# A two-block transformer kernel: residual spread over tiles, later products, fewer mask passes

## The chip, the cores and the metric

The kernel runs on one core of a Trainium2 chip as one launch. The metric is the device time of the launch in microseconds. Engines are named as in the profile: PE (matrix products), DVE, ACT, POOL (elementwise work) and SP (which issues the DMA transfers).

## The reference

Everything is float32, with 1024 rows of width 1024. Two blocks follow each other.

```python
# block 1
mod = silu(c) @ w_mod + b_mod            # six vectors: sh1, sc1, g1, sh2, sc2, g2
z = (x*(1+sc1) + sh1) @ w_in             # feeds four mixers
y = concat(mlstm(z), sgu(z), conv(z), s5(z)) @ w_out
x = layer_norm(ALPHA*x + g1*y, ln1_w, ln1_b)
x = layer_norm(ALPHA*x + g2*swiglu(x*(1+sc2)+sh2), ln2_w, ln2_b)   # hidden width 2816
# block 2
proj = rms_norm(x) @ w_in_2              # 3512 columns
ret  = group_norm(retention(q, k, v)) * silu(r_g)          # 8 heads of 64
sel  = top_k(indexer_score(i_q, i_k, i_w), 256)            # per query, causal by chunks of 64
dsa  = softmax over the selected keys, 8 heads, latent keys/values, * silu(d_g)
x = x + concat(ret, dsa) @ w_out_2
x = x + sigmoid(rms_norm(x) @ w_ple_gate) * (p @ w_ple_proj)
out = rms_norm(x)
```

The S5 mixer is a complex linear recurrence in both directions over 16 groups of 16 channels. Where more than 256 keys can be seen by a query, those with the 256 highest indexer scores count, ties going to the lower key.

## The kernel before

Each float32 product is made of three PE products of split operands (high by high, low by high, high by low): lines 184 to 186 for one order of operands and 195 to 197 for the other. `k.split` makes the two parts of a weight page: the high part on ACT (L173), the low part, `raw - high`, on DVE (L174). Weights arrive in 3 `raw` buffers; 46 pages of 128 x 1024 float32 serve all other tiles; PSUM has 4 banks in a pool `mm` and 4 in a pool `ax`.

The program is written as Python generators. `merge` and `pipe` run them a step at a time, and a `yield` ends a step; so the place of an instruction in the program follows from the number of yields before it. A scheduler then orders the instructions of each engine by their place in the program, and may run a later one first where the earlier is not ready.

**Stage A (0 to about 640 us)** works out the modulation vectors, the mixers and LN1. `mod_rest` adds up eight products of a `w_mod` page by a scalar on DVE (`macc`, L1317) and then sums over partitions on PE with a column of ones (L1324), for four vectors. Each of the 16 `s5_group`s multiplies on PE, scans and rotates on DVE and POOL, makes `sr` and `si` (L2147, L2148) on DVE, ends its step, and adds three products on PE (L2153 to L2155). `s5_groups` loads T for each quad of groups and LO and E for each half quad just before they are used.

**Stage B (640 to 1350)** is the FFN. `Ffn.half(j, h)` makes hidden tile j for half h of the rows. In blocks of two hidden tiles, `stage_b` makes the halves, multiplies the rows of w_ffn_out by g2 on POOL (L395), splits them, and adds their products to the eight tiles `acc[t]` of the stream (PE L184 to L186 into `ax`, DVE L429). After block 0's weights, the eight tiles are turned into the residual: L407 multiplies by `ALPHA*ln1_w` on DVE, L408 adds `ALPHA*ln1_b` on DVE and POOL in turns; both vectors are loaded and scaled (L402, L405) just before.

**Stage C (1350 to 2160)** is block 2. `retention_pair` (L870 to L915) makes for each tile t a projection in an `mm` bank, rotates it on DVE and POOL (`rA`), transposes it on PE into an `ax` bank (L888, L889), and makes scores (`st`, two `ax` banks), output (`po`, L906/L907) and state (`pn`), one `ax` bank each. Behind it, as background work, `search` finds each query's 256th score by bisection on DVE (L763) and ACT, and the mask loop turns scores into 0 or 1e30 for tiles 2 to 7, in six steps of passes over the tile, all on DVE: L803 (count over a threshold), L805 and L806 (least score at or under it), L813 (count again), L816 (equal), L818 (running count), L820, L821 and L823 (the mask). The sparse attention of a tile (`head`) makes logits (L1149, L1150) plus mask (L1151), exponentials, transposes (L1161), and the value products L1177 for two heads at a time (`AVB = 2`), at the end of every second head.

Of the kernel before, what the change touches and what calls it, by code (L numbers as in the profile page):

```python
# [10 lines left out]
F32 = mybir.dt.float32  # L11
# [40 lines left out]
AVB = 2  # L52
# [319 lines left out]
def stage_b(k, ffn, acc, mod_s, ln1_w, ln1_b, w_fo, ln2_w, ln2_b, x2_s, sink, early, pre_sink, after, background, spare):  # L372
# [3 lines left out]
    FB = 2  # L376
    for b0 in range(0, NF, FB):
# [3 lines left out]
        for j in blk:  # L381
            for h in range(2):
                if j or h:
                    for _ in ffn.half(j, h):
                        pass
            acts.append(ffn.a.pop(j))
            del ffn.w[j]
        if b0 == 0:
            g2b = page("g2b")
            k.bcast(g2b, mod_s, 5120, 1024)  # L390
# [8 lines left out]
        if b0 == 0:  # L399
            aw = page("aw")  # L400
            k.bcast(aw, ln1_w, 0, 1024)
            nc.gpsimd.tensor_scalar(aw, aw, ALPHA, None, op0=ALU.mult)  # L402
            ab = page("ab")
            k.bcast(ab, ln1_b, 0, 1024)
            nc.gpsimd.tensor_scalar(ab, ab, ALPHA, None, op0=ALU.mult)  # L405
            for t in range(8):
                nc.vector.tensor_tensor(acc[t], acc[t], aw, op=ALU.mult)  # L407
                (nc.vector if t % 2 else nc.gpsimd).tensor_tensor(acc[t], acc[t], ab, op=ALU.add)  # L408
# [43 lines left out]
BIG = 1.0e30  # L452
MAGIC = 12582912.0
# [58 lines left out]
class StageC:  # L512
# [223 lines left out]
    def search(self):  # L736
# [7 lines left out]
        act_tiles = {2, 3, 4, 5}  # L744
# [48 lines left out]
    def masks(self):  # L793

        k, nc, n_sel, th = self.k, self.k.nc, 256, self.th
        for j, t in enumerate(range(2, 8)):
# [6 lines left out]
            nc.vector.tensor_scalar(a[:, :w], x, T, None, op0=ALU.is_gt, op1=ALU.add, accum_out=c[:, 0:1])  # L803
            yield 1
            nc.vector.tensor_scalar(a[:, :w], x, T, 3.0e38, op0=ALU.is_le, op1=ALU.mult)  # L805
            nc.vector.tensor_tensor_reduce(e[:, :w], x, a[:, :w], 1.0, 3.0e38, op0=ALU.add, op1=ALU.min, accum_out=c[:, 1:2])  # L806
            yield 1

            nc.vector.tensor_scalar(c[:, 2:3], c[:, 0:1], n_sel - 0.5, None, op0=ALU.is_gt)
            v = k.sm.tile([128, 1], F32, name="tkv", bufs=2)  # L810
            nc.vector.tensor_copy(v, T)
            nc.vector.copy_predicated(v, c[:, 2:3].bitcast(I32), c[:, 1:2])
            nc.vector.tensor_scalar(a[:, :w], x, v, None, op0=ALU.is_gt, op1=ALU.add, accum_out=c[:, 0:1])  # L813
            nc.vector.tensor_scalar(c[:, 3:4], c[:, 0:1], -1.0, float(n_sel), op0=ALU.mult, op1=ALU.add)
            yield 1
# [1518 lines left out]
```

## Time and profile before

| | |
|---|---|
| time, median of 3 runs | 2163.7 us (2162.11 to 2166.16) |
| the profiled execution | 2162.43 us, span 2160.4 us |
| PE busy | 2027.2 us, 94% of the span |
| DVE, ACT, POOL busy | 1291.4, 790.5 and 403.4 us |
| mean granted PE clock | 0.972 |

The span is what the profiler saw of the engines; the other 2.0 us of the profiled execution lie around it. A row of the timeline gives the start, the duration, the engine, the line, and in square brackets how long the engine had idled before and what ended that. A row of the waits is a sum over the whole run.

### The profile page before, as it was taken

What the parts mean: (1) busy time and instruction counts of PE and PEld (TensorE: products, weight loads), DVE (VectorE), ACT (ScalarE), POOL (GpSimd) and SP (SyncE); (2) the same over time, 40 slices, a digit from 0 to 9 for tenths busy, and PEclk for the clock granted to TensorE, in tenths of its full rate; (3) what the DMA queues carried; (4) which work ended last, traced back from release to release, by engine and by line L of the source; (5) the groups of instructions that cost most, each with busy time, mean ns of one, the idle gap of its engine ahead of it and who ended that gap; (6) DMA issues with size and microseconds to landing.
All of it is one profiled execution on the core that took longest, in us unless ns stands there. A gap on an engine that the chain in (4) does not pass through costs nothing. (4 is left out here: it accounts for less than half of the span.)

```text
span 2160.4 us, 29069 instructions
## 1 busy us (share of the span) xinstructions
PE 2027.2 (94%) x10808; PEld 1671.3 (77%) x10808; DVE 1291.4 (60%) x2652; ACT 790.5 (37%) x1570; POOL 403.4 (19%) x455
## 2 busy tenths in 40 slices
PE   8897898899997999999999999999999897999998
PEld 3797887777876888888887788786777785778886
DVE  6967725476666534555346454757888556966533
ACT  2522224343131222222222221545887434345432
POOL 1464403112024000000000001430002121000032
PEclk9999899989999999999999999999999998999999
DMA  8464564356411235554335543313312205343611
GB/s 288 158 161 144 149 194 166 129 167 219 171 49 59 100 113 200 187 202 162 128 140 205 186 160 116 142 40 108 142 50 89 88 24 161 133 151 115 222 59 69
DMA packets 144334, 299.32 MB, mean 139 GB/s; under 512 B 30648, under 2 KB 70072, under 8 KB 144192
## 3 DMA queue, kind: packets, MB, share of 16 engines
q1 hardware_dynamic: 144192, 297.46, 40.8%
q8 instruction: 85, 1.39, 0.3%
q14 instruction: 57, 0.47, 0.1%
HBM read 208.81 MB, written 87.56 MB: 137 GB/s over the span
## 5 line engine op out<-in xcount | busy, mean ns | idle before, releaser
L195 PE MATMUL mm<-hh,whi 128*128 128x512 f32 x704 | 275.2, 391 | 5.0 <-ACT whi L173 5.0
L197 PE MATMUL mm<-hh,wlo 128*128 128x512 f32 x704 | 274.9, 390 | 0.9 <-DVE wlo L174 0.9
L196 PE MATMUL mm<-hl,whi 128*128 128x512 f32 x704 | 274.9, 390 | 0.0
L184 PE MATMUL mm<-whi,xTh 128*128 128x512 f32 (+1 forms) x576 | 227.9, 400 | 2.9 <-DMA whi<-scr_wsp 1.7
L185 PE MATMUL mm<-wlo,xTh 128*128 128x512 f32 (+1 forms) x576 | 226.0, 394 | 0.8 <-DMA wlo<-scr_wsp 0.8
L186 PE MATMUL mm<-whi,xTl 128*128 128x512 f32 (+1 forms) x576 | 224.5, 393 | 0.0
L174 DVE TENSOR_TENSOR wlo<-raw,whi 128x1024 fp32r<-128x1024 f32 (+2 forms) x99 | 121.7, 1249 | 126.4 <-ACT whi L173 126.0
L395 POOL TENSOR_TENSOR raw<-raw,g2b 128x1024 f32<-128x1024 f32 x22 | 55.1, 2506 | 595.9 <-DMA raw<-in_w_ffn_out 552.5
L195 PEld LDWEIGHTS mm<-hh,whi 128*128 128x128 f32 x704 | 132.6, 188 | 33.1 <-ACT whi L173 5.9
L184 PE MATMUL mm<-whi,hhi 128*128 128x256 f32 (+1 forms) x512 | 150.6, 294 | 5.0 <-DVE csg L1515 3.4
L197 PEld LDWEIGHTS mm<-hh,wlo 128*128 128x128 f32 x704 | 132.5, 188 | 29.2 <-DVE wlo L174 1.9
L196 PEld LDWEIGHTS mm<-hl,whi 128*128 128x128 f32 x704 | 132.6, 188 | 27.5
L184 PE MATMUL ax<-whi,ah 128*128 128x512 f32 x352 | 138.4, 395 | 15.2 <-DVE acc L429 15.2
L186 PE MATMUL mm<-whi,hlo 128*128 128x256 f32 (+1 forms) x512 | 148.8, 292 | 1.9 <-POOL hlo L1359 1.5
L185 PE MATMUL mm<-wlo,hhi 128*128 128x256 f32 (+1 forms) x512 | 149.0, 291 | 0.0
L429 DVE TENSOR_TENSOR acc<-ax,acc 128x512 f32<-128x512 f32 x176 | 116.3, 684 | 38.8 <-PE ax L186 38.2
L185 PE MATMUL ax<-wlo,ah 128*128 128x512 f32 x352 | 138.0, 392 | 0.0
L186 PE MATMUL ax<-whi,al 128*128 128x512 f32 x352 | 137.9, 392 | 0.0
L367 DVE TENSOR_TENSOR sg<-mm,sg 128x512 f32<-128x512 f32 x44 | 30.4, 691 | 170.4 <-PE mm L197 159.6
L173 ACT ACTIVATE whi<-raw 128x1024 fp32r<-128x1024 f32 (+2 forms) x99 | 100.7, 1046 | 85.1 <-DMA raw<-in_w_fi_o 62.9
L184 PEld LDWEIGHTS mm<-whi,xTh 128*128 128x128 f32 x576 | 109.1, 190 | 27.9 <-DMA whi<-scr_wsp 3.7
L185 PEld LDWEIGHTS mm<-wlo,xTh 128*128 128x128 f32 x576 | 109.5, 190 | 20.2 <-DMA wlo<-scr_wsp 1.4
(615 smaller groups left out, 4476.0 us busy)
## 6 DMA issues: line engine op xcount, KB each, us to landing
raw<-in_w_fi_o SPq DMA_DIRECT2D x44, 512.0 KB, 5.6
wmr<-in_w_mod SPq DMA_DIRECT2D x32, 512.0 KB, 6.4
raw<-in_w_in_2o SPq DMA_DIRECT2D x24, 512.0 KB, 5.4
scr_wsp<-phi SPq DMA_DIRECT2D x24, 512.0 KB, 3.8
scr_wsp<-plo SPq DMA_DIRECT2D x24, 512.0 KB, 4.2
whi<-scr_wsp SPq DMA_DIRECT2D x24, 512.0 KB, 6.1
wlo<-scr_wsp SPq DMA_DIRECT2D x24, 512.0 KB, 6.7
raw<-in_w_ffn_out SPq DMA_DIRECT2D x22, 512.0 KB, 3.7
```

Source lines behind the costliest of these rows:

```text
L173: nc.scalar.activation(hi, raw, AF.Copy)
L174: nc.vector.tensor_tensor(lo, raw, hi, op=ALU.subtract)
L184: nc.tensor.matmul(ps, ah, bh, start=k == 0, stop=False)
L185: nc.tensor.matmul(ps, ah, bl, start=False, stop=False)
L186: nc.tensor.matmul(ps, al, bh, start=False, stop=k == n - 1)
L195: nc.tensor.matmul(ps, ah, bh, start=k == 0, stop=False)
L196: nc.tensor.matmul(ps, ah, bl, start=False, stop=False)
L197: nc.tensor.matmul(ps, al, bh, start=False, stop=k == n - 1)
L367: nc.vector.tensor_tensor(sg, pu, sg, op=ALU.mult)
L395: nc.gpsimd.tensor_tensor(raw, raw, g2b, op=ALU.mult)
L429: nc.vector.tensor_tensor(v[:, cs], ps, v[:, cs], op=ALU.add)
```

## The change

Seven places change:

- `stage_b`: the residual moves into a generator, `residual()`, that is stepped while block 0's halves are made (three steps in each of the three halves, whose products are yielded in pieces of 2 for that). All eight additions are on POOL; `aw` and `ab` are loaded first.
- `s5_group`: one more step before the products L2153 to L2155.
- `mod_rest`: `2 * MR` (6) units of steps before the sum L1324.
- `s5_groups`: T, LO and E are loaded one group ahead.
- the mask loop: for tiles 6 and 7 the first count and the search for the least score are left out (the threshold is used as it is); for all tiles the equality pass goes to POOL and yields 2^100, and the last three passes become two, so 5 passes for two tiles and 7 for four.
- `AVB` is 4: the value products of four heads follow each other.
- `retention_pair`: the transposed tile `pt` is in `mm`, not in `ax`.

```diff
--- before.py
+++ after.py
@@ -49,7 +49,7 @@
 RA, RB = 2, 1
 WQ, KEYS = 3, 6
 HA, HB, OA, OB = 2, 3, 4, 3
-AVB = 2
+AVB = 4
 RETS = [(0, 1), (0, 4), (0, 7), (1, 2), (1, 5), (2, 0), (2, 3), (2, 6)]
 DSAS = [(4, 4), (5, 0), (5, 4), (6, 0), (6, 4), (7, 0), (7, 2)]
 LOADS = {(3, 0): 1, (3, 2): 1, (3, 4): 1, (3, 6): 1, (7, 1): 1, (7, 3): 1, (7, 5): 1, (7, 7): 1}
@@ -374,6 +374,20 @@
     nc, page = k.nc, k.page
     NF = DFF // 128
     FB = 2
+
+    def residual():
+
+        aw, ab = page("aw"), page("ab")
+        for p, w in ((aw, ln1_w), (ab, ln1_b)):
+            k.bcast(p, w, 0, 1024)
+            nc.gpsimd.tensor_scalar(p, p, ALPHA, None, op0=ALU.mult)
+        yield 1
+        for t in range(8):
+            nc.vector.tensor_tensor(acc[t], acc[t], aw, op=ALU.mult)
+            nc.gpsimd.tensor_tensor(acc[t], acc[t], ab, op=ALU.add)
+            yield 1
+
+    res = residual()
     for b0 in range(0, NF, FB):
         blk = list(range(b0, min(NF, b0 + FB)))
         last = blk[-1] == NF - 1
@@ -381,10 +395,13 @@
         for j in blk:
             for h in range(2):
                 if j or h:
-                    for _ in ffn.half(j, h):
-                        pass
+                    for n, _ in enumerate(ffn.half(j, h, 8 if b0 else 2)):
+                        if b0 == 0 and n % 3 == 0:
+                            next(res, None)
             acts.append(ffn.a.pop(j))
             del ffn.w[j]
+        for _ in res:
+            pass
         if b0 == 0:
             g2b = page("g2b")
             k.bcast(g2b, mod_s, 5120, 1024)
@@ -396,16 +413,6 @@
             hl = page("whi", F32R), page("wlo", F32R)
             k.split(*hl, raw)
             wf.append(hl)
-        if b0 == 0:
-            aw = page("aw")
-            k.bcast(aw, ln1_w, 0, 1024)
-            nc.gpsimd.tensor_scalar(aw, aw, ALPHA, None, op0=ALU.mult)
-            ab = page("ab")
-            k.bcast(ab, ln1_b, 0, 1024)
-            nc.gpsimd.tensor_scalar(ab, ab, ALPHA, None, op0=ALU.mult)
-            for t in range(8):
-                nc.vector.tensor_tensor(acc[t], acc[t], aw, op=ALU.mult)
-                (nc.vector if t % 2 else nc.gpsimd).tensor_tensor(acc[t], acc[t], ab, op=ALU.add)
         if b0:
             for _ in range(PS):
                 next(spare, None)
@@ -450,6 +457,7 @@
 
 
 BIG = 1.0e30
+OFF = 2.0 ** 100
 MAGIC = 12582912.0
 TWO_PI = 2.0 * math.pi
 
@@ -741,7 +749,7 @@
             nc.gpsimd.memset(self.sc[t], 0.0)
             nc.gpsimd.memset(self.sc[t][:64, t * 128 + 64:], BIG)
         tl = list(range(2, 8))
-        act_tiles = {2, 3, 4, 5}
+        act_tiles = self.act_tiles = {2, 3, 4, 5}
         key = k.ctile([128, 6], "tkey", I32)
         xm = k.ctile([128, 6], "txor", I32)
         thr = k.ctile([128, 6], "tthr")
@@ -800,27 +808,29 @@
             a = k.page("tka")
             e = k.page("tke")
             c = k.sm.tile([128, 4], F32, name="tkc", bufs=2)
-            nc.vector.tensor_scalar(a[:, :w], x, T, None, op0=ALU.is_gt, op1=ALU.add, accum_out=c[:, 0:1])
-            yield 1
-            nc.vector.tensor_scalar(a[:, :w], x, T, 3.0e38, op0=ALU.is_le, op1=ALU.mult)
-            nc.vector.tensor_tensor_reduce(e[:, :w], x, a[:, :w], 1.0, 3.0e38, op0=ALU.add, op1=ALU.min, accum_out=c[:, 1:2])
-            yield 1
-
-            nc.vector.tensor_scalar(c[:, 2:3], c[:, 0:1], n_sel - 0.5, None, op0=ALU.is_gt)
-            v = k.sm.tile([128, 1], F32, name="tkv", bufs=2)
-            nc.vector.tensor_copy(v, T)
-            nc.vector.copy_predicated(v, c[:, 2:3].bitcast(I32), c[:, 1:2])
-            nc.vector.tensor_scalar(a[:, :w], x, v, None, op0=ALU.is_gt, op1=ALU.add, accum_out=c[:, 0:1])
-            nc.vector.tensor_scalar(c[:, 3:4], c[:, 0:1], -1.0, float(n_sel), op0=ALU.mult, op1=ALU.add)
-            yield 1
-            nc.vector.tensor_scalar(e[:, :w], x, v, None, op0=ALU.is_equal)
+            if t in self.act_tiles:
+                nc.vector.tensor_scalar(a[:, :w], x, T, None, op0=ALU.is_gt, op1=ALU.add, accum_out=c[:, 0:1])
+                yield 1
+                nc.vector.tensor_scalar(a[:, :w], x, T, 3.0e38, op0=ALU.is_le, op1=ALU.mult)
+                nc.vector.tensor_tensor_reduce(e[:, :w], x, a[:, :w], 1.0, 3.0e38, op0=ALU.add, op1=ALU.min, accum_out=c[:, 1:2])
+                yield 1
+
+                nc.vector.tensor_scalar(c[:, 2:3], c[:, 0:1], n_sel - 0.5, None, op0=ALU.is_gt)
+                v = k.sm.tile([128, 1], F32, name="tkv", bufs=2)
+                nc.vector.tensor_copy(v, T)
+                nc.vector.copy_predicated(v, c[:, 2:3].bitcast(I32), c[:, 1:2])
+            else:
+                v = T
+
+            nc.gpsimd.tensor_scalar(e[:, :w], x, v, OFF, op0=ALU.is_equal, op1=ALU.mult)
+            nc.vector.tensor_scalar(a[:, :w], x, v, None, op0=ALU.is_le, op1=ALU.add, accum_out=c[:, 0:1])
+            nc.vector.tensor_scalar(c[:, 3:4], c[:, 0:1], OFF, (n_sel - w) * OFF, op0=ALU.mult, op1=ALU.add)
+            yield 1
             z = k.zero1.to_broadcast([128, w])
             nc.vector.tensor_tensor_scan(x, e[:, :w], z, 0.0, op0=ALU.add, op1=ALU.add)
             yield 1
             nc.vector.scalar_tensor_tensor(x, x, c[:, 3:4], e[:, :w], op0=ALU.is_le, op1=ALU.mult)
-            nc.vector.tensor_tensor(x, x, a[:, :w], op=ALU.add)
-            yield 1
-            nc.vector.tensor_scalar(x, x, -BIG, BIG, op0=ALU.mult, op1=ALU.add)
+            nc.vector.scalar_tensor_tensor(x, a[:, :w], OFF, x, op0=ALU.mult, op1=ALU.subtract)
             self.done.add(('mask', t))
             yield 1
 
@@ -884,7 +894,7 @@
             ts = slice(t * 128, t * 128 + 128)
             nc.scalar.activation(sg[:, ts], ps[:, 384:512], AF.Silu, scale=self.rr[:, t:t + 1])
             yield from steps(RA)
-            pt = k.ax.tile([128, 2, 128], F32, name="ax")
+            pt = k.mm.tile([128, 2, 128], F32, name="mm")
             nc.tensor.transpose(pt[:, 0], qk[:, 0:2].rearrange("p h d -> p (h d)"), k.ident)
             nc.tensor.transpose(pt[:, 1], qk[:, 2:4].rearrange("p h d -> p (h d)"), k.ident)
             nc.scalar.activation(qt[:, 0], pt[:, 0], AF.Copy, scale=0.125)
@@ -1318,6 +1328,7 @@
                 yield MR
             o = k.page("mro")
             nc.sync.dma_start(o[:1], dap(I['b_mod'], cb * 1024, [[0, 1], [1, 1024]]))
+            yield 2 * MR
             for g in range(2):
                 cs = slice(g * 512, g * 512 + 512)
                 ps = k.ax.tile([128, 512], F32, name="ax")
@@ -2106,18 +2117,28 @@
 
     def s5_groups(self):
         k, nc, S = self.k, self.k.nc, self.S
-        py = {}
-        for q in range(4):
-            T = k.page("s5T", shape=[128, 848])
-            nc.sync.dma_start(T, dap(S['seq'], q * 960, [[16, 8], [3840, 16], [1, 848]]))
-            for hf in range(2):
-                LO = k.page("s5LO", shape=[128, 2, 2, 2, 128])
-                nc.sync.dma_start(LO.rearrange("p a i g c -> p (a i g c)"), dap(S['s5lo'], (q * 2 + hf) * 131072, [[1024, 128], [1, 1024]]))
-                E = k.page("s5E", shape=[128, 2, 2, 192])
-                nc.sync.dma_start(E.rearrange("p g i x -> p (g i x)"), dap(S['s5e'], (q * 4 + hf * 2) * 384, [[6144, 128], [1, 768]]))
-                for g2 in range(2):
-                    g = hf * 2 + g2
-                    yield self.s5_group(q, g, LO[:, 0, :, g2], LO[:, 1, :, g2], T[:, g * 240:g * 240 + 128], E[:, g2], py)
+        py, T = {}, {}
+
+        def load(n):
+            q, hf = divmod(n, 2)
+            if hf == 0:
+                T[q] = k.page("s5T", shape=[128, 848])
+                nc.sync.dma_start(T[q], dap(S['seq'], q * 960, [[16, 8], [3840, 16], [1, 848]]))
+            LO = k.page("s5LO", shape=[128, 2, 2, 2, 128])
+            nc.sync.dma_start(LO.rearrange("p a i g c -> p (a i g c)"), dap(S['s5lo'], (q * 2 + hf) * 131072, [[1024, 128], [1, 1024]]))
+            E = k.page("s5E", shape=[128, 2, 2, 192])
+            nc.sync.dma_start(E.rearrange("p g i x -> p (g i x)"), dap(S['s5e'], (q * 4 + hf * 2) * 384, [[6144, 128], [1, 768]]))
+            return LO, E
+
+        ahead = load(0)
+        for n in range(8):
+            q, hf = divmod(n, 2)
+            LO, E = ahead
+            for g2 in range(2):
+                g = hf * 2 + g2
+                if g2 and n < 7:
+                    ahead = load(n + 1)
+                yield self.s5_group(q, g, LO[:, 0, :, g2], LO[:, 1, :, g2], T[q][:, g * 240:g * 240 + 128], E[:, g2], py)
 
     def s5_group(self, q, g, L, O, T, e, py):
         k, nc = self.k, self.k.nc
@@ -2147,6 +2168,7 @@
         nc.vector.tensor_tensor(sr, d[:, 0], d[:, 1], op=ALU.add)
         nc.vector.tensor_tensor(si, sp[:, 1], sp[:, 0], op=ALU.subtract)
         yield 1
+        yield 1
         if g == 0:
             py[q] = k.mm.tile([128, 4, 128], F32, name="mm")
         p = py[q]
```

## Rows read from the trace of the kernel before

**Rows 1.** The page, part 1: busy us, share of the span, instructions.

```profile
PE 2027.2 (94%) x10808; PEld 1671.3 (77%) x10808; DVE 1291.4 (60%) x2652; ACT 790.5 (37%) x1570; POOL 403.4 (19%) x455
```

**Rows 2.** Windows: start:end, us, busy us of each engine (instructions), PEclk, DMA share, GB/s.

```profile
180.00:210.00 30.00, 21.96 (x152) 19.40 (x151) 24.29 (x48) 6.82 (x9) 14.42 (x19) 1.00 0.55 158
...
1800.00:1900.00 100.00, 86.59 (x433) 65.73 (x434) 79.20 (x181) 39.43 (x95) 6.47 (x3) 0.88 0.53 179
...
1920.00:2040.00 120.00, 119.42 (x911) 99.56 (x912) 72.50 (x191) 59.39 (x113) 4.17 (x4) 1.00 0.42 138
```

**Rows 3.** Waits of PE over the run: us in total, times, longest us.

```profile
PE ax L184 <- DVE acc L429: 15.2, 3, 12.0
PE mm L2154 <- DVE s5A L2147: 12.5, 8, 2.2
PE ax L888 <- DVE ro L907: 9.0, 5, 4.7
PE ax L1324 <- DVE macc L1317: 7.0, 2, 6.0
...
PE ax L2127 <- DMA s5LO<-scr_s5lo: 0.8, 3, 0.4
```

**Rows 4.** Timeline of PE, FFN block 0.

```profile
698.02 0.80 PE L184 MATMUL ax<-whi,ah 128*128 128x512 f32 x1 [11.96 <-DVE acc L429]
...
701.56 0.40 PE L184 MATMUL ax<-whi,ah 128*128 128x512 f32 x1
701.79 0.40 PE L185 MATMUL ax<-wlo,ah 128*128 128x512 f32 x1
```

**Rows 5.** Timeline of SP, DVE and POOL around the residual.

```profile
614.88 26.78 SPq L394 DMA_DIRECT2D raw<-in_w_ffn_out  x2
...
654.89 0.69 DVE L367 TENSOR_TENSOR sg<-mm,sg 128x512 f32<-128x512 f32 x1 [8.87 <-PE mm L197]
...
669.33 3.72 POOL L402 TENSOR_SCALAR aw<-aw 128x1024 f32<-128x1024 f32 x1 [15.57 <-DMA aw<-in_ln_w]
...
673.08 6.52 DVE L407 TENSOR_TENSOR acc<-acc,aw 128x1024 f32<-128x1024 f32 x3 [2.68 <-POOL aw L402]
679.52 1.21 DVE L408 TENSOR_TENSOR acc<-acc,ab 128x1024 f32<-128x1024 f32 x1
```

**Rows 6.** Timeline of PE at the other stalls and at one value burst.

```profile
229.48 0.49 PE L2154 MATMUL mm<-s5LO,s5A 128*128 128x128 f32 x2 [2.15 <-DVE s5A L2147]
...
359.80 3.57 PE L1324 MATMUL ax<-macc,ones 128*1 128x512 f32 x4 [6.04 <-DVE macc L1317]
...
1701.75 0.45 PE L888 MATMUL ax<-ident,rA 128*128 128x128 f32 x1 [4.72 <-DVE ro L907]
...
1869.77 0.80 PE L186 MATMUL mm<-whi,yohl 128*128 128x512 f32 x1 [2.35 <-DVE yohl L1115]
...
2024.16 1.97 PE L1177 MATMUL ax<-L,V 128*64 128x128 f32 x32
```

**Rows 7.** Timeline of DVE, mask passes of tiles 6 and 7.

```profile
1867.37 1.75 DVE L820 SCALAR_TENSOR_TENSOR score<-score,tkc,tke 128x896 f32<-128x896 f32 x1
...
1879.77 1.27 DVE L803 TENSOR_SCALAR_CACHE_REDUCE tka<-score,tth 128x1024 f32<-128x1024 f32 x1
...
1883.30 1.21 DVE L806 CUSTOM_DVE_ANT_0 tke<-score,tka 128x1024 f32<-128x1024 f32 x1
...
1887.38 0.75 DVE L816 TENSOR_SCALAR tke<-score,tkv 128x1024 f32<-128x1024 f32 x1
```

**Rows 8.** Single lines: duration in ns, min/median/max, first and last start.

```profile
L407 DVE TENSOR_TENSOR acc<-acc,aw x8: 1211/3356/3410, 673.1 to 694.0; 128x1024 f32<-128x1024 f32 x8
...
L408 POOL TENSOR_TENSOR acc<-acc,ab x4: 2637/3188/3247, 675.9 to 693.1; 128x1024 f32<-128x1024 f32 x4
```

**Rows 9.** Line L1177: durations as in 8; idle of its engine before it, us, times.

```profile
L1177 PEld LDWEIGHTS ax<-L,V x576: 132/137/231, 1819.3 to 2047.1; 128*64 128x64 f32 x192
...
  issue: 6.7, 28
```

## The prediction

> **What bounds the kernel now.** I read the page's first part first: PE is busy for 2027.2 of 2160.4 us and no other engine for more than 60% [rows 1]. So PE sets the end, and a change that leaves PE's products as they are can win only what PE loses: 133 us of idle time, and the time in which it runs at the lower of its two clock levels behind a gap. Then the windows, to see where this lies: 13 us between 1800 and 1900 at a granted clock of 0.88, 8 us in the 30 us from 180, and next to nothing (0.6 us) in the 120 us from 1920 [rows 2]. Then PE's waits, which name who was late: DVE, in all four of the largest waits that the change touches, 43.7 us together [rows 3]. Last the timeline at the places themselves, for what comes ahead of the late instruction and what the clock does behind the gap [rows 4 to 7]. The reader is to see that DVE is never full for long, but that its queue is in order: a pass of 1 to 3 us at the wrong moment makes PE wait.
>
> **The residual (FFN block 0).** PE stands for 11.96 us before the first output product that needs a free `ax` bank; the bank comes free when DVE adds into `acc`, and DVE is busy with L407 and L408 until then [rows 4, 5]. Behind the gap the clock is at the lower level: the eight products from 698.02 take 3.54 us, where two neighbours at the higher level start 0.23 us apart [rows 4]; eight of those are 1.84, so 1.7 us more. Some 13.6 us can be had. The change moves the 16 passes ahead, into the time of the three halves, where DVE has little to do (an idle stretch of 8.87 us ends at 654.89 [rows 5]). What it adds: nothing in passes, but four additions move from DVE at 1.21 us [rows 5] to POOL at 3.19 us [rows 8]. POOL then has, in the 36 us between the end of the transposes at about 633 and 669, where it began before [rows 5]: eight additions at 3.19 (25.5 us), two scalings at 3.72 at most (7.4 us), two products of weights, priced as additions (6.4 us): 39.3 us. It is full and overruns by some 3.3 us. Everything in POOL's queue behind an addition waits with it: the products `raw * g2b`, then the splits on DVE and ACT, then block 0's output products. SP's queue: `aw` and `ab` are now issued ahead of the two weight loads that hold SP from 614.88 to 641.66 [rows 5], so they land early. I take -10 us: 13.6 less the overrun. Bounds: -13.6 (all hidden) and +4 (a new stall of one add in front of each of the two low parts that L174 makes, and of the weights' product).
>
> DVE's L407 takes 1.21 us alone and 3.36 us at the median, beside POOL's additions [rows 8]: the two take turns. The Trainium skill says so too (GPSIMD Engine Reference, section 8, Key points): POOL shares its SBUF interfaces with DVE and gets in the way of DVE instructions with two SBUF operands, and elementwise work is about twice as fast on DVE. By that rule the four additions moved to POOL speak against this part; by the row they cost POOL's time only as long as DVE has slack.
>
> **S5 products a step later.** PE waits 12.5 us in eight waits for L2147 [rows 3], the worst kind as in [rows 6]: 2.15 us, and the DVE rows ahead of it are scans. One step more lets PE take other products first. Bounds: -12.5, and 0 if PE has nothing else or the next thing is as late. In this stretch PE is busy 21.96 us of 30 and DVE 24.29 [rows 2]: DVE is close behind as a limit, so a wait that goes here may reappear at the next DVE result. I take a third: -4.
>
> **Modulation sums later.** The two waits for `macc` are 7.0 us, one of them 6.04 [rows 3, 6], and the four sums behind it are slow too (3.57 us). After 6 more units DVE's last L1317 should be done. Who waits for the sum: DVE's L1325 and a transfer to memory, needed first much later. Bounds -7.0 and 0, taken: -4, since DVE's queue can be late by more than the step.
>
> **S5 loads ahead.** LO is last in three short waits, 0.8 us together [rows 3]. I take -1; +4 if the pages that are held longer (three of 46 for a half quad) make another load late; SP's queue is in order, so a load that waits for a page holds those behind it.
>
> **Mask passes.** At tile 7 DVE loses L803 (1.27), L805 (one operand, priced as L816 at 0.75), L806 (1.21), L816 (0.75, to POOL), and of the last three passes one (L823, priced as L816): 4.7 us [rows 7]. Tile 6, by its width, 4.1 us. Tiles 2 to 5 lose L816 and one of the last passes, 1.5 us at full width; their widths sum to 2.25 of 1024: 3.4 us. Together 12.2 us of DVE time, none of it on PE. What PE gets: the 13.4 us lost in 1800 to 1900 [rows 2] hold 2.35 us of direct wait behind L818 and L820 (1.75 us beside a POOL pass) and the low clock after it [rows 6, 7]. Added: the equality pass on POOL; no such row. Below, 0.75 us as on DVE; above, 3.72 us as L402 [rows 5, 7]. It is nearest to L402 (one operand, a scalar, POOL). Over the six widths (4.125 of 1024) that is at most 15.3 us, and if DVE stood still for all of it, 3.1 us worse than before. The scan waits for it; `e` is not needed by anything else, and L813 fills part of the wait. I take -5, bounds -12.2 and +3.1.
>
> **Value products of four heads.** Ahead of its bursts the engine idles 6.7 us in 28 cases with no releaser named [rows 9], 0.24 us a burst: 16 bursts fewer give 3.8 us, in a stretch where PE is never idle [rows 2]. A burst of 32 products is 1.97 us [rows 6]; now two such follow each other, and logits for the next head come 2 us later. Four pages are held instead of two. I take -4, bounds -4 and +4.
>
> **`pt` in `mm`.** L888 waits for L907 because both want an `ax` bank: 9.0 us, with one wait of 4.72 and the lower clock behind it, as in [rows 4] ([rows 3, 6]). In `mm` the wait for L907 goes, but `pt` and the projections then share four banks, and PE can be fewer tiles ahead. Taken: -2; bounds -11 (9.0 and 2 for the clock) and +5, one such wait more.
>
> **Sum**: -10 -4 -4 -1 -5 -4 -2 = -30, from the profiled execution's 2162.4 us (2160.4 of span and 2.0 around it) 2132.4. The median of the runs shown is 1.3 us above that execution, so 2133.7, rounded 2134. Bounds that could hold together: the low ends of the four largest parts (-13.6, -12.5, -12.2, -11) cannot all be had.
>
> **Rivals.**
> - *The residual's stall comes back* (0.13). POOL is full in 633 to 669; if the weights' low parts are queued behind the adds, PE waits there instead. Against it: DVE's idle rows. +4 in place of -10: 2134 + 14 = 2148.
> - *Stage A is bound by DVE* (0.10): DVE at 24.29 of 30 beside PE's 21.96 [rows 2]. The 9 us of S5 and modulation don't reach the end: 2143.
> - *POOL and DVE take turns in the masks* (0.12): +3.1 in place of -5: 2142. The 1.75 us of L820 beside a POOL pass speaks for it [rows 7]. The Trainium skill's page named above says elementwise work is better on DVE; by it this rival is the likely course, and the trace agrees as far as L407 shows it.
> - *`mm` is short in retention* (0.10), the one that ends slower. 32 items each have a projection and a `pt` in four banks; if each waits as the five waits for L907 do on average, 1.8 us, that is 58 us: 2134 + 2 + 58 = 2194. It decides from 0.9 us an item (28 us) on. Against it: a projection's bank is read within the same step.
> - *More than the sum* (0.05): stalls go with their low clock: about 2118.
>
> **How the numbers follow.** The forecast holds with 0.50; its own range is 2124 to 2144. The first three rivals end at 2142 to 2148; two of them together reach 2155 to 2157. A change is told from none at 0.2%, 4.3 us. Faster: 0.50 + 0.13 + 0.10 + 0.12 + 0.05 less 0.06 for rivals that come together, 0.84. Same: 0.06 and a hundredth of the slower rival, 0.07. Slower: 0.09. The range for 8 in 10 reaches from 2113 (below the fifth rival) to 2165 (rivals together, and the start of the fourth).
>
> **What would show it.** No wait of PE at `ax` for L429 in FFN block 0 and granted clock 1.0 there; waits for L2147 and `macc` gone from the list; L1177 in groups of up to 64; DVE's busy time 12 us down, POOL's 16 to 28 us up (12.8 of additions and 3 to 15 of passes); PE's busy time about the same and its idle time down by 30 us. The prediction is wrong if a wait for `wlo`, for `mm` at a projection, or for the new POOL pass appears with more than 5 us in total, or if PE's busy time rises, since then the clock took back what the waits gave.

## The result and the profile after

| | before | after |
|---|---|---|
| time, median | 2162.9 us (2162.1 to 2166.2, 4 runs) | 2136.3 us (2131.8 to 2141.3, 4 runs) |
| ratio, 95% interval | | 0.9875 (0.9849 to 0.9900) |
| profiled execution, span | 2162.4, 2160.4 us | 2141.3, 2139.5 us |
| PE, DVE, POOL busy | 2027.2, 1291.4, 403.4 us | 2019.0, 1281.4, 429.0 us |

The kernel is faster by 26.6 us at the medians. The time forecast was 2134, the measured one is 2136.3. The profiled execution is the slowest of the four; the same kernel run again gave 2135.2 us (2134.6 to 2137.7) where the kernel before took 2167.3 beside it, ratio 0.9857 (0.9841 to 0.9873), and its profiled execution has a span of 2132.9.

The waits of PE after, in us in total, times and longest:

```profile
PE ax L2148 <- DMA s5LO<-scr_s5lo: 15.3, 4, 7.2
...
PE ax L184 <- ACT whi L173: 5.7, 1, 5.7
...
PE ax L184 <- DVE acc L436: 3.2, 2, 2.6
...
PE mm L2177 <- DVE s5A L2169: 1.6, 2, 0.8
...
PE ax L1335 <- DVE macc L1327: 0.9, 1, 0.9
...
PE mm L2176 <- DVE s5A L2168: 0.3, 1, 0.3
```

Of the four waits in [rows 3] that the change was to remove, three are nearly gone: L2154's (now L2176) from 12.5 to 0.3 us, with 1.6 us at the product behind it (L2177), L888's for `ro` (L907) from the list altogether, L1324's (now L1335) from 7.0 to 0.9. The first, for `acc`, fell from 15.2 to 3.2: the one of 12.0 in FFN block 0 is gone, and the two that are left stand behind the FFN's last product of a hidden tile, with 3.2 us before as after. Two are new at the head: 15.3 us for the S5 loads, and 5.7 us for weights in FFN block 0. Over the whole span PE idles for 120.5 us instead of 133.2 (117.9 in the second execution) and is busy for 8.2 us less (12.2 in the second); its mean granted clock is 0.971 (0.973), where it was 0.972.

FFN block 0 after, PE, POOL and DVE (compare [rows 4, 5]), then the weight products on POOL before:

```profile
661.82 0.39 PE L197 MATMUL mm<-hh,wlo 128*128 128x512 f32 x1
667.87 2.07 PE L184 MATMUL ax<-whi,ah 128*128 128x512 f32 x4 [5.67 <-ACT whi L173]
...
671.20 0.63 PE L184 MATMUL ax<-whi,ah 128*128 128x512 f32 x1
...
674.50 0.40 PE L185 MATMUL ax<-wlo,ah 128*128 128x512 f32 x1
...
634.97 6.55 POOL L387 TENSOR_TENSOR acc<-acc,ab 128x1024 f32<-128x1024 f32 x2
644.49 2.71 POOL L387 TENSOR_TENSOR acc<-acc,ab 128x1024 f32<-128x1024 f32 x1 [2.96 <-DVE acc L386]
648.42 16.01 POOL L387 TENSOR_TENSOR acc<-acc,ab 128x1024 f32<-128x1024 f32 x5 [1.23 <-DVE acc L386]
664.40 4.65 POOL L412 TENSOR_TENSOR raw<-raw,g2b 128x1024 f32<-128x1024 f32 x2
...
644.87 14.55 DVE L386 TENSOR_TENSOR acc<-acc,aw 128x1024 f32<-128x1024 f32 x5
```

```profile
649.01 4.74 POOL L395 TENSOR_TENSOR raw<-raw,g2b 128x1024 f32<-128x1024 f32 x2 [16.32 <-DMA g2b<-scr_mod]
```

The gap is 5.67 us instead of 11.96, and another operand ends it: `whi`, made from `raw * g2b` (L412), which POOL takes up at 664.40, behind the last of its eight additions. Before the change POOL did these weight products first, from 649.01, and the additions later. The eight additions take 2.7 to 3.4 us each, DVE's multiplications beside them 2.9 (14.55 us for five); POOL's own work from the first scaling (629.32) to the second weight product (669.05) is 35.5 us, and for 4.2 us it waits for DVE's multiplications. PE has run out of products of hidden tiles at 662.2; before the change they lasted to 686.1. The products behind the gap are at the lower clock again (0.63 us long; 0.40 from 674.50), now for 6.6 us, where it was 3.5 [rows 4].

The masks after, the new pass on POOL and DVE's scan behind it:

```profile
1832.45 3.28 POOL L825 TENSOR_SCALAR tke<-score,tth 128x896 f32<-128x896 f32 x1
1838.87 3.71 POOL L825 TENSOR_SCALAR tke<-score,tth 128x1024 f32<-128x1024 f32 x1 [3.14 <-DVE tkc L827]
...
1839.00 2.86 DVE L830 TENSOR_TENSOR_SCAN score<-tke,zero 128x896 f32<-128x896 f32 x1
...
1848.23 2.28 DVE L830 TENSOR_TENSOR_SCAN score<-tke,zero 128x1024 f32<-128x1024 f32 x1
```

The equality pass takes 3.71 us at 1024 columns, five times the 0.75 that DVE took for the comparison alone [rows 7] (0.74 for the whole pass, in experiment 10), and the scan that runs beside it 2.86 us at 896 columns, where it took 1.97 before the change. A tile keeps four passes on DVE (tiles 6 and 7) or seven (the others), and each has one on POOL: 5 and 8 in all, where the list of the change has 5 and 7.

**Stretches.** Whole times differ from run to run by more than most parts are worth. So I read each part from the stretch in which it acts, between two events that every version has; the windows below start and end there. Stage A is read from the first S5 product (L2127 before) to the last LN1 transposition (L334), the FFN from there to the last product of a hidden tile (L197), the retention from the first to the last transposition at L888, and the attention from there to the last value product. Kernels that do not differ in a stretch agree within 1.4 us in the attention and within 2.6 in the FFN and the retention: the FFN is 706.32 us in both executions of the changed kernel, but 704.1 in the one of experiment 4; before the change it is 710.6, and 708.2 in that of experiment 5. A part of under 3 us can't be read there from one execution. Stage A is 468.4 to 468.9 us in four kernels that have none of the changes to it, and 456.6 to 462.3 in those that have all three as in the change.

### The profile page after: what moved, and what is told of

Same layout as the page of the kernel before. It is cut to its first block, busy times and chain, and to the rows that moved or that the text cites. A ratio compares the mean times of both kernels' runs of the same rounds, so it can differ in the third digit from the quotient of the medians.

```text
span 2139.5 us, 29059 instructions
## 1 busy us (share of the span) xinstructions
PE 2019.0 (94%) x10808; PEld 1673.6 (78%) x10808; DVE 1281.4 (60%) x2620; ACT 785.4 (37%) x1568; POOL 429.0 (20%) x465
## 5 line engine op out<-in xcount | busy, mean ns | idle before, releaser
L197 PE MATMUL mm<-hh,wlo 128*128 128x512 f32 x704 | 275.1, 391 | 1.4 <-DVE wlo L174 1.4
L185 PE MATMUL mm<-wlo,xTh 128*128 128x512 f32 (+1 forms) x576 | 225.2, 392 | 2.5 <-DMA wlo<-scr_wsp 2.5
L186 PE MATMUL mm<-whi,xTl 128*128 128x512 f32 (+1 forms) x576 | 223.7, 391 | 0.0
L174 DVE TENSOR_TENSOR wlo<-raw,whi 128x1024 fp32r<-128x1024 f32 (+2 forms) x99 | 126.0, 1293 | 129.4 <-ACT whi L173 128.7
L412 POOL TENSOR_TENSOR raw<-raw,g2b 128x1024 f32<-128x1024 f32 x22 | 54.1, 2463 | 597.2 <-DMA raw<-in_w_ffn_out 569.6
L197 PEld LDWEIGHTS mm<-hh,wlo 128*128 128x128 f32 x704 | 132.5, 188 | 30.0 <-DVE wlo L174 2.7
L186 PE MATMUL mm<-whi,hlo 128*128 128x256 f32 (+1 forms) x512 | 149.6, 293 | 1.9 <-POOL hlo L1370 1.5
L186 PE MATMUL ax<-whi,al 128*128 128x512 f32 x352 | 138.3, 393 | 0.0
L185 PEld LDWEIGHTS mm<-wlo,xTh 128*128 128x128 f32 x576 | 109.3, 190 | 22.5 <-DMA wlo<-scr_wsp 3.6
```

Of the source, the lines that this page charges most:

```text
L174: nc.vector.tensor_tensor(lo, raw, hi, op=ALU.subtract)
L185: nc.tensor.matmul(ps, ah, bl, start=False, stop=False)
L186: nc.tensor.matmul(ps, al, bh, start=False, stop=k == n - 1)
L197: nc.tensor.matmul(ps, al, bh, start=False, stop=k == n - 1)
L412: nc.gpsimd.tensor_tensor(raw, raw, g2b, op=ALU.mult)
```

## The experiments

**1. The changed kernel again.** No edit.

> The changed kernel once more, unaltered. It was 26.6 us under the kernel before at the medians, while its profiled execution, the slowest of its four, was 21 us under it and stood 15.3 us for S5's LO loads. Theory L (the spread of the changed kernel's runs, 2131.8 to 2141.3, is the LO wait, which varies with when the loads land): this profile has another sum for that wait, and its span follows it roughly one for one. Rival: the wait is again 14 to 16 us and the span differs for another reason. Time expected: 2136, with 2131 to 2141 as its runs' spread.

Measured: 2135.2 us; LO waits 14.1 us where they were 15.3, span 2132.9 where it was 2139.5. Theory L falls: the wait moved by 1.2 us and the span by 6.6. Some 3.3 us of it lie before the first S5 product (165.1 against 161.8 us), in the opening, and 2.7 us between it and the last LN1 transposition (windows under experiments 2 to 4). What makes this spread was not tried.

**2 to 4. S5's two parts, alone and together taken out.** No loads ahead (`no_d`), no later products (`no_b`), neither (`no_bd`), the edit shortened:

```diff
-        ahead = load(0)                  # no_d, no_bd: T, LO and E loaded
+            T = k.page("s5T", ...)       #   in the loop, just ahead of use
...
         yield 1
-        yield 1                          # no_b, no_bd
         if g == 0:
             py[q] = k.mm.tile(...)
```

> The changed kernel with S5's loads where they were before (just ahead of the half quad that uses them); the later products stay. Theory D (the loads a group ahead make the LO waits, since SP issues in order and a load that waits for a page holds the next): PE's waits for LO fall from 15.3 us to under 3, time about 8 us under the changed kernel, near 2128. Rival B (the products a step later make them, by keeping the pages of S5 longer): the waits for LO stay above 8 us, and the time is the same or some us more, 2136 to 2145.

> The changed kernel with S5's products where they were before (one step earlier); the loads a group ahead stay. Theory D (loads ahead make the LO waits): LO waits stay above 8 us, and the waits for L2147's result (12.5 us before) come back beside them, so the time is 5 to 10 us more than the changed kernel's, 2141 to 2146. Rival B (the later products make the LO waits): LO waits under 3 us, waits for sr and si near 12 us, time within 4 us of 2136.

> The changed kernel with S5 as before: products a step earlier, loads just ahead of use. Theory X (what the later products won, 12.5 us of waits for sr and si, the waits for LO took back, so both parts together are worth nothing): time 2133 to 2138, as the changed kernel. Rival S (they still bring a good part of what stage A gained, the modulation sums the rest): 2140 to 2145.

Measured: without the loads ahead 2136.3 us (ratio 0.9856), without the later products 2138.3 (0.9871), without both 2145.1 (2142.9 to 2154.2; ratio 0.9914, 0.9898 to 0.9930). The stretch from the first S5 product to the last LN1 transposition, in this order: before, after, after again, no loads ahead, no later products, neither (start and end, length, busy us of PE, PEld, DVE, ACT, POOL, clock, DMA share, GB/s):

```profile
161.50:630.27 468.77, 424.57 (x2641) 371.63 (x2640) 301.54 (x626) 140.34 (x256) 122.17 (x157) 0.94 0.48 156
...
165.10:626.82 461.72, 419.89 (x2641) 370.78 (x2640) 302.31 (x626) 137.74 (x254) 120.59 (x157) 0.94 0.50 160
...
161.80:620.86 459.06, 419.18 (x2641) 370.34 (x2640) 302.61 (x626) 137.47 (x254) 120.67 (x157) 0.94 0.50 161
...
163.70:624.17 460.47, 423.03 (x2641) 373.19 (x2640) 302.01 (x626) 140.88 (x257) 123.98 (x157) 0.94 0.50 162
...
166.50:627.29 460.79, 420.89 (x2641) 369.21 (x2640) 300.39 (x626) 137.56 (x254) 123.37 (x157) 0.95 0.49 160
...
167.20:636.24 469.04, 425.57 (x2641) 371.86 (x2640) 302.88 (x626) 140.37 (x256) 122.37 (x157) 0.95 0.49 159
```

Neither part: 469.0, as before the change (468.8). Either one: 460.5 or 460.8. Both: 461.7 and 459.1. And PE's waits without the loads ahead, without the later products, and without both:

```profile
PE ax L2138 <- DMA s5LO<-scr_s5lo: 8.1, 2, 7.3
PE mm L2166 <- DVE s5A L2158: 6.8, 5, 2.8
...
PE ax L2148 <- DMA s5LO<-scr_s5lo: 9.5, 4, 5.3
...
PE mm L2175 <- DVE s5A L2168: 2.7, 3, 1.7
...
PE mm L2165 <- DVE s5A L2158: 12.6, 9, 2.4
...
PE ax L2138 <- DMA s5LO<-scr_s5lo: 1.8, 2, 1.6
```

So theory D and rival B both fall: each part alone has LO waits of 8 to 10 us, and both together 14 to 15. Theory X falls as well: with neither there is 12.6 us of waiting for `sr` and hardly any for LO, with both the reverse, and yet both are worth 8 us of the stretch and about 10 of the time. In the length of the stage the two parts are substitutes, one is enough. A sum of waits does not tell what they are worth; part of it (2.5 to 6.4 us) is in PE's busy time (425.6 against 419.2 to 423.0).

The stretch, cut at the last S5 product (L2155 before), shows that they win in different places (us):

| | to the last S5 product | from there on |
|---|---|---|
| before | 107.6 | 361.2 |
| neither | 109.9 | 359.2 |
| loads ahead alone (`no_b`) | 95.5 | 365.3 |
| later products alone (`no_d`) | 111.3 | 349.2 |
| both (the two executions) | 105.2, 105.2 | 356.5, 353.9 |

The loads ahead shorten the first piece, in which PE idles for 14.1 us instead of 19.6, and the later products the second, 18.2 us instead of 24.6. Why the two gains do not add up is not settled.

**5. Modulation sums alone.** The kernel before with one line more:

```diff
+            yield 2 * MR
             for g in range(2):
                 cs = slice(g * 512, g * 512 + 512)
```

> The kernel before with the sums of the modulation vectors six units later, nothing else. Reading Z (from the changed kernel without S5's two parts, whose stage A from the first S5 product to the end of the transpositions is as long as before, 469.0 against 468.8 us): the waits for macc go from 7.0 to 3 us or less and nothing is won, because the time is given back at other waits for DVE in the stage; time within 2 us of the kernel before. Reading of the prediction: 4 us less, both in this stretch and in the time.

Measured: ratio 1.0001 (0.9988 to 1.0013). The waits for `macc` went from 7.0 to 2.6 us, and the stretch of stage A became longer, 472.6 us against 468.8, which is outside the 468.4 to 468.9 of kernels without this part. That is one execution, though: the kernel of experiment 4, which has the later sums too, has 469.0. The stretch and two of its waits:

```profile
164.00:636.63 472.63, 429.20 (x2641) 374.55 (x2640) 302.42 (x626) 140.32 (x256) 123.80 (x157) 0.94 0.48 155
...
PE mm L2155 <- DVE s5A L2148: 12.0, 8, 2.4
...
PE ax L1325 <- DVE macc L1317: 2.6, 1, 2.6
```

Reading Z holds here: by itself this part wins nothing.

**6. Additions shared.** The changed kernel, the residual's additions on DVE and POOL in turns, as they had been before:

```diff
             nc.vector.tensor_tensor(acc[t], acc[t], aw, op=ALU.mult)
-            nc.gpsimd.tensor_tensor(acc[t], acc[t], ab, op=ALU.add)
+            (nc.vector if t % 2 else nc.gpsimd).tensor_tensor(acc[t], acc[t], ab, op=ALU.add)
```

> The changed kernel with the residual's additions on DVE and POOL in turns, as before the change, and all else as changed. Theory P (POOL's queue sets the gap that is left in FFN block 0: the products of w_ffn_out by g2 start at 664.4, behind the last addition, and PE stands 5.7 us for the parts made of them): POOL has four additions of 2.7 to 3.2 us less, the weight products start 6 us or more earlier, the gap is under 1 us, time about 7 us under the changed kernel. Rival T (DVE and POOL take turns on the same tiles, so what POOL sheds DVE pays): the gap stays above 4 us and the time within 3 us of the changed kernel's.

Measured: 2125.6 us (2124.0 to 2131.7), ratio 0.9813 (0.9798 to 0.9828), some 10 us under the changed kernel on the same chip. PE and POOL at the gap, then the FFN's stretch before, after and in this kernel:

```profile
661.96 0.50 PE L185 MATMUL ax<-wlo,ah 128*128 128x512 f32 x1 [2.71 <-DVE wlo L174]
...
631.01 3.23 POOL L387 TENSOR_TENSOR acc<-acc,ab 128x1024 f32<-128x1024 f32 x1
...
653.52 6.71 POOL L412 TENSOR_TENSOR raw<-raw,g2b 128x1024 f32<-128x1024 f32 x2
```

```profile
630.27:1340.85 710.58, 692.68 (x3038) 571.51 (x3037) 342.43 (x412) 172.82 (x229) 75.13 (x30) 0.99 0.43 151
...
626.82:1333.14 706.32, 694.61 (x3037) 572.36 (x3037) 341.88 (x408) 172.94 (x229) 86.26 (x34) 0.99 0.43 150
...
622.86:1325.32 702.46, 693.82 (x3038) 571.94 (x3037) 347.74 (x412) 173.04 (x229) 74.81 (x30) 0.99 0.43 151
```

Theory P holds, rival T does not: with four additions instead of eight, POOL takes up the weight products 22.5 us after its first addition where it took 29.4 (653.52 less 631.01; 664.40 less 634.97), and the gap is 2.71 us, now at the low part on DVE, so not under 1 us as the theory had it. The FFN is 8.1 us shorter than before instead of 4.3. The theory expected about 7 us in the time; of the 10 measured 3.9 are in the FFN. Where the rest of the difference in time is, the trace does not tell: the profiled execution was this kernel's slowest.

**7. Masks alone.** The kernel before with the mask loop of the change (the hunks from `OFF` to the end of the loop).

> The kernel before with the mask passes alone changed (5 or 7 of 9, the equality pass on POOL). The changed kernel is 10.7 us shorter between its first and last value product than the kernel before. Theory M (as predicted: DVE's passes are what PE stands for between 1800 and 1900): this stretch is 5 to 8 us shorter, and so is the time, near 2160 where the kernel before takes 2165. Rival V (the bursts of value products carry nearly all of it): the stretch is under 2 us shorter. Rival T (POOL and DVE take turns): the stretch is longer by 1 to 3 us.

**8. Value products alone.** The kernel before with `AVB = 4`.

> The kernel before with the value products of four heads following each other, and nothing else changed. Theory of the prediction: a quarter of a microsecond for each of 16 bursts that go, 3.8 us; nothing from other effects; so the stretch from the first scores of the attention to the last value product is 3.5 to 4.5 us shorter, and the time 4 us. Rival V (fewer switches also spare waits for the transposed pages): 6 to 9 us. Rival H (four pages held and longer bursts make the logits late): 0 or longer.

Measured: masks 2162.3 us, ratio 0.9989 (0.9978 to 0.9999), values 2158.0, ratio 0.9969 (0.9954 to 0.9984). The expectations named the first value product and the first scores as boundaries, but with bursts of four heads the first value product comes 4.3 us later by itself; so both are read on one stretch, from the last retention transposition to the last value product. Before, masks alone, values alone, the changed kernel (its second execution):

```profile
1785.37:2047.52 262.15, 244.11 (x1618) 194.83 (x1618) 178.10 (x418) 119.59 (x250) 15.62 (x13) 0.95 0.47 155
...
1786.69:2044.76 258.07, 240.70 (x1618) 193.20 (x1618) 166.99 (x388) 119.56 (x250) 29.38 (x18) 0.96 0.47 158
...
1786.26:2042.32 256.06, 235.73 (x1618) 192.65 (x1618) 176.52 (x418) 118.74 (x250) 16.55 (x13) 0.95 0.48 159
...
1766.79:2020.32 253.53, 236.27 (x1618) 194.69 (x1618) 166.60 (x388) 118.30 (x250) 30.30 (x18) 0.94 0.49 160
```

Masks 4.1 us (DVE's busy time there 11 us less, POOL's 14 more); values 6.1; both in the changed kernel 8.6. Where it is, by line, in that stretch (busy us and mean ns of one; idle us before), before and then values alone:

```profile
L186 PE MATMUL mm<-whi,yohl 128*128 128x512 f32 x120 | 48.3, 408 | 2.4 <-DVE yohl L1115 2.4
L1177 PE MATMUL ax<-L,V 128*64 128x128 f32 x576 | 46.7, 282 | 1.3 <-DVE L L1166 0.8 <-ACT L L1164 0.5
L1161 PE MATMUL ax<-ident,L 128*128 128x128 f32 x288 | 45.0, 280 | 3.8 <-ACT L L1153 2.9 <-DVE ql L1048 0.5 <-DVE L L1166 0.2
```

```profile
L1161 PE MATMUL ax<-ident,L 128*128 128x128 f32 x288 | 43.5, 279 | 6.5 <-ACT L L1153 5.0 <-DVE ql L1048 0.5 <-ACT L L1164 0.4
L1177 PE MATMUL ax<-L,V 128*64 128x128 f32 x576 | 37.5, 278 | 1.1 <-DVE L L1166 0.6 <-ACT L L1164 0.5
```

The 576 value products keep PE busy for 37.5 us instead of 46.7, 9.2 us less. The times of neighbouring groups overlap, so the window is the surer measure: PE is busy for 8.4 us less in the stretch (235.73 against 244.11). In PE's timeline the value products stand in 22 groups instead of 47, for other products had stood inside the bursts too: some 0.3 us of busy time for each of 25 groups that went. Little of it is clock, since the mean of one product is 282 ns before and 278 after. Of this 2.7 us come back as idle time in front of the transpositions (3.8 to 6.5 us), most of it waits for the exponentials. In the kernel with the masks alone the 2.4 us in front of L186 are gone:

```profile
L186 PE MATMUL mm<-whi,yohl 128*128 128x512 f32 x120 | 47.0, 396 | 0.1
```

But idle time comes back there too: 3.4 us in front of the value products (1.3 before) and 5.4 in front of the transpositions (3.8). PE idles for only 0.7 us less in the stretch; the other 3.4 of the 4.1 us are busy time (240.70 against 244.11), with products that are shorter on the mean (L186 396 ns, before 408; granted clock 0.96, before 0.95).

So the masks bring less than theory M's 5 to 8 us, but twice what rival V allowed, and rival T falls. For the value products the low end of rival V is met in number, but not its reason: the waits for transposed pages did not shrink. The masks' ratio alone hardly leaves 1, since a gain of 4 us is within the runs' spread; the stretch shows it.

**9. `pt` in `mm`, alone.**

```diff
-            pt = k.ax.tile([128, 2, 128], F32, name="ax")
+            pt = k.mm.tile([128, 2, 128], F32, name="mm")
```

> The kernel before with the transposed tile of the retention in the other pool of banks, nothing else changed. The changed kernel is 6.1 us shorter between its first and last transposition of this kind. Theory G (this part carries it; the wait for the output's bank goes, and no wait for the projections' banks takes its place): the stretch is 4 to 7 us shorter, the time 4 to 6 us. Rival of the prediction (the projections' banks run short): the stretch is longer, and waits of PE for a bank of the projections appear. Rival M (the masks' fewer passes carry it, since they begin in the last pair): under 2 us.

Measured: 2157.4 us (2157.2 to 2158.1), ratio 0.9965 (0.9952 to 0.9979). From the first to the last of these transpositions, before and in this kernel:

```profile
1554.05:1785.37 231.32, 220.58 (x1135) 179.86 (x1136) 162.34 (x479) 138.40 (x396) 40.23 (x41) 0.98 0.18 59
...
1554.07:1779.24 225.17, 221.12 (x1149) 181.60 (x1150) 163.94 (x481) 138.17 (x398) 40.38 (x41) 0.98 0.18 60
...
PE ax L904 <- DVE rst L914: 3.1, 1, 3.1
...
PE mm L888 <- POOL rA L567: 1.8, 1, 1.8
```

231.3 us became 225.2; the changed kernel has the same 225.2. Kernels with `pt` in `ax` have 229.1 to 231.3 and those with `pt` in `mm` 225.1 to 226.2, so the part is worth 3 to 6 us there. Theory G holds, if less surely in its size. The wait for `ro` is gone, no wait for a bank of the projections is in the list, and what L888 still waits for is its own input (1.8 us). The stretch behind it is 1.2 us longer (263.3 against 262.2).

**10. Equality pass on DVE**, in the changed kernel: `nc.gpsimd.tensor_scalar(e ...)` became `nc.vector.tensor_scalar(e ...)`.

> The changed kernel with the equality pass of the masks on DVE in place of POOL. As predicted (the pass is worth taking off DVE): the stretch between first and last value product is 1 to 3 us longer than the changed kernel's 217.5, time 2136 to 2138. Rival T (POOL and DVE take turns, so the pass on POOL costs DVE and the scan behind it as much as it spares): the stretch is the same or up to 3 us shorter.

Measured: 2137.9 us, ratio 0.9868 (0.9849 to 0.9887), from the changed kernel not to be told. Between first and last value product 218.8 us against 217.4, 1.3 us longer; on the wider stretch 254.7 against 253.5:

```profile
1769.01:2023.71 254.70, 236.34 (x1619) 193.57 (x1618) 168.17 (x393) 118.56 (x250) 14.56 (x13) 0.95 0.49 160
```

This is not told from nothing: kernels with the pass on POOL have 217.4 to 218.6 us on the one stretch and 253.5 to 254.3 on the other. POOL takes 15.9 us for what DVE does in about 3, and DVE stands 5.6 us for it in four waits of the scan; by these runs the pass on POOL wins some 1 us at most, and perhaps nothing. The reading of the prediction is met at its low end by the one comparison, but not clear of the scatter; rival T's loss does not show either, so the two stay undecided.

**11. S5's loads issued by ACT**, on top of the shared additions (`nc.sync.dma_start` in `load` became `nc.scalar.dma_start`, three places).

> The changed kernel with the residual's additions shared between DVE and POOL (2125.6 us), and with S5's loads of T, LO and E issued by ACT in place of SP. Theory Q (the loads are late because SP issues in order and stands for a weight buffer or a store ahead of them): waits of PE for LO go from 13.6 us to under 4, the stretch from the first S5 product to the end of the transpositions is 3 to 8 us shorter than 456.6, time 2118 to 2123. Rival P (the loads wait for their pages, whoever issues them, and ACT's other work now stands behind them): the waits for LO stay above 8 us and the time is the same or up to 10 us longer.

Measured: 2132.3 us (2127.9 to 2132.5), ratio 0.9835 (0.9819 to 0.9851); with SP it was 0.9813. PE's waits for LO are 10.5 us in five, the stretch is 455.9 us:

```profile
PE ax L2148 <- DMA s5LO<-scr_s5lo: 10.5, 5, 4.7
```

Theory Q falls, rival P's marks are there. SP's order alone does not make the loads late.

**12. Shared additions without the later modulation sums** (the line `yield 2 * MR` taken out of experiment 6's kernel).

> The changed kernel with the residual's additions shared (2125.6 us) and with the sums of the modulation vectors where they were before. Reading Z (the later sums are worth nothing, with S5's parts as without them): the waits for macc come back with 5 to 7 us, yet the time stays within 3 us of 2125.6, and the stretch from the first S5 product to the end of the transpositions within 3 us of 456.6. Reading W (the later sums only pay once S5's parts have moved PE's other waits): time 2129 to 2133.

Measured: 2134.5 us (2134.2 to 2135.9), ratio 0.9858 (0.9839 to 0.9877) against 0.9813 with the line. The waits for `macc` are back with 7.3 us; the stretch is 461.1 us:

```profile
164.80:625.86 461.06, 419.87 (x2641) 369.84 (x2640) 299.42 (x626) 140.41 (x256) 119.62 (x157) 0.94 0.50 160
...
PE ax L1334 <- DVE macc L1327: 7.3, 2, 6.1
```

The time, past the upper end of reading W's range, speaks for W and against Z: worthless alone, the later sums bring several microseconds once S5's parts are in. The stretch does not decide it: 461.1 is 4.5 us over that of experiment 6, but inside the 456.6 to 462.3 that kernels with all three parts showed. The two were timed on different chips, so this stays open.

## Why the prediction was right

The sum was -30 us and the measured difference -26.6 (-32 in the second set of runs). The terms were not as good as the sum: all but that of the masks were off by half or more, in both directions, and that they cancelled is luck: the residual fell short by some 6 us and the modulation sums, alone, by 4; S5's parts and `pt` gave some 3 and 4 us more than was taken.

- **What bounds the kernel**: right in that PE sets the end. But idle time was to fall by 30 us at about the same busy time; it fell by 12.7 (15.3 in the second execution), and busy time by 8.2 (12.2). Most of that is not time at the lower clock, as the prediction had it: in the attention busy time fell by 7.7 us at a granted clock of 0.94, before 0.95. Breaks between groups of products, which it did not count, are a third thing that PE loses (experiment 8).
- **Residual, -10**: mis-sized; it brought -4.3 in the FFN, at most some 7 with the scatter of that stretch. The sentence that POOL "is full and overruns by some 3.3 us", and that the weight products wait behind the additions, named the right mechanism, but it was charged as 3.3 us of the old stall. What it makes is a stall of its own: 5.67 us and the lower clock behind it. The sum gave POOL until 669, but PE had nothing else from 662.2 on; and it put at nothing POOL's waits for DVE's multiplications, 4.2 us, while POOL's own work was 35.5 us and not 39.3. With half of the additions on DVE (experiment 6) the part brings 8.1. The Trainium skill (GPSIMD Engine Reference, section 8, Key points), which holds POOL the slower place for elementwise work and in DVE's way, agrees with this: additions took 2.7 to 3.4 us on POOL against 1.21 on DVE alone [rows 5].
- **S5, -4 and -1**: mis-sized; -8 in the stretch, about -10 in the time, and the two are not a sum: each alone brings it, in different places. That LO "is last in three short waits" did not last: 14 to 15 us of LO waits appeared, and yet no loss by them can be shown.
- **Modulation sums, -4**: not borne out alone (0); beside S5's parts between 0 and some 9, open.
- **Masks, -5**: right, -4.1 alone. The dearer end for the POOL pass (3.72 us) was the right one, 3.71. DVE did stand 5.6 us for it, yet without it on POOL the stretch is no shorter (experiment 10). DVE's busy time fell by 10.0 us (5.0 in the second execution; 12.2 worked out; 11.1 in the attention with the masks alone), POOL's rose by 25.6 (16 to 28).
- **Value products, -4**: mis-sized; -6.1. The price of a burst, 0.24 us, was read from [rows 9], and that row is of the weight loads (PEld), whose idle time is not PE's; PE's own idle time in front of the value products is 1.3 us in all. What the bursts cost is busy time of PE, 8.4 us of the stretch, with 2.7 us given back in front of the transpositions. That the size came out right is luck.
- **`pt` in `mm`, -2**: mis-sized; -6.1 (3 to 6 with the scatter), of which 1.2 comes back later. The list of waits (9.0 us) was a better guide than the fear for `mm`'s banks.
- **The rivals**: the residual's stall did come back in part, 5.7 us in block 0, by the very queue that it named. The prediction's own sign of being wrong, over 5 us of waits for `wlo`, was met in substance, for the wait is for `whi` of the same page. POOL and DVE taking turns in the masks: the turns are there (scan 2.86 us where it takes 1.97), a loss in the time isn't. `mm` short in retention: no such wait. Stage A bound by DVE: the S5 part was worth more than forecast, so no.

## What to carry to other kernels

Where work is moved to a queue with room, look at what stands behind it there: an addition on POOL that costs nothing itself held the weights that PE needed next, and leaving half of them on DVE was worth as much again as the move. Judge a part by the stretch between two events in which it acts: parts of 4 to 6 us that whole times could not tell apart could be read from single executions, once other kernels had shown how far the stretch scatters (up to 2.6 us here). Look which engine a row of idle time belongs to: that of the weight loads is not PE's. Do not add up waits on a list as gains: two edits may each remove the same loss, and a wait that appears may cost nothing.

The best version measured is that of experiment 6, 2125.6 us, in one set of five runs.

## What the runs showed of the hardware

A comparison with one value per row and a multiplication, over 128 rows, takes POOL 3.28 us at 896 columns and 3.71 at 1024; on DVE they are 0.68 and 0.74 (experiment 10). A scan on DVE beside it took 2.86 us at 896 columns, where it took 1.97 before the change, and 2.28 at 1024 once POOL was done. A break between two groups of value products cost PE some 0.3 us of busy time (8.4 us for 25 groups that went), which no list of waits shows.
